# Key low parts zero-padded to 128 rows in the score matmuls of a differential attention

## The chip, the cores and the metric

The kernel runs on one core of a Trainium2 chip. The metric is the device time of one execution in microseconds (us), as the median over runs: 940.03 us for the kernel before, from 3 runs between 939.41 and 940.34.

## What is computed

One hybrid decoder layer in float32, with 512 tokens and a model width of 2048. One input projection feeds three branches: differential attention (8 heads), a state space mixer and an attention into 256 memory tokens. Their gated outputs go through one output projection, a norm and the residual. The change touches the differential attention. Each head has two components c of 64 query and key features, and 128 value features:

```python
s = einsum('bhcqd,bhckd->bhcqk', q_blk, k) * 64 ** -0.5     # c = 0, 1; d = 64
p = softmax(where(causal, s, -inf), axis=-1)
a = p[:, :, 0] - lam * p[:, :, 1]
o = einsum('bhqk,bhkv->bhqv', a, v)
o = rms_norm(o, diff_subln_w) * (1.0 - lambda_init)
```

## The kernel before, in words

Every large product is made in a reduced-precision float32 form (fp32r): each operand is split into a high part that fits the form and a low part that holds the rest, and three matmuls (high by high, high by low, low by high; the helper `mm3`, L95 to L97) give the product. Weights come from memory as chunks of 512 KB by the SP queue (`load_chunk`, L215). ScalarE makes the high part (L247, tile `whi`), VectorE subtracts it from the chunk to make the low part (`sub_hi`, L100, tile `wlo`). Three raw chunks and two split ones are held at a time. `dense_ws` makes one block of 128 output features by 512 tokens in 48 matmuls of 512 columns; `dense_xs` makes the values `v` with matmuls of 256 columns.

The differential attention works on four pairs of heads. For each pair the values, then two blocks q and two blocks k are projected. `rope` (L738 and below) rotates a block: ScalarE copies it out of PSUM into `raw` (L740), four small transfers on the SP queue fetch the swapped halves into `sw` (L743), GpSimd (POOL) multiplies both by the tables (L744, L745), and VectorE adds them (L746). The result is then laid out in a tile `pair` of two slots, one per component. For q, slot c holds in one half of the 128 rows the high part of component c and in the other half its low part. For k, both halves of slot c hold the high part of component c, half of them copied by POOL (L755, L756). So one matmul over 128 rows (L777) makes q-high by k-high and q-low by k-high together. What is missing is q-high by k-low. Before the change, `kl` holds the low parts of both components in one tile of 512 columns, component 0 in rows 0 to 63 and component 1 in rows 64 to 127, and a second matmul over those 64 rows (L780) adds it to the same PSUM bank.

In `head`, the score tile of query block i (i = 0 to 3) and component c has (i+1)*128 columns. So one head has eight L777 matmuls and eight L780 matmuls, two of each width 128, 256, 384 and 512, and the eight heads have 64 of each. After them VectorE masks and finds the maximum (L781, L782), ScalarE takes the exponential (L787), VectorE normalises and combines the two components (L790 to L793), TensorE transposes (L797), and the result is split (L798, L100) for the product with v (tile `av`). The tail of a head copies `av` out (L807), takes the sum of squares and scales.

The order of the instructions on each engine is set when the program is built, by a scheduler that interleaves independent work: the score matmuls of one pair of heads stand singly or in small groups between the projection matmuls of the next pair (`v`, `q`, `k`), and those of the last pair between the projections of the gates (`dg`).

Of the kernel before, what the change touches and what calls it, by code (L numbers as in the profile page):

```python
# [11 lines left out]
F32 = mybir.dt.float32  # L12
F32R = mybir.dt.float32r
BF16 = mybir.dt.bfloat16
I32 = mybir.dt.int32
AF = mybir.ActivationFunctionType
ALU = mybir.AluOpType
AX = mybir.AxisListType
PSUM = bass.MemoryType.PSUM

P = 128
D = 2048
S = 512
# [13 lines left out]


def _digits(value, widths):
    """value as a sum of float32 parts of the given numbers of bits."""  # L40
    from fractions import Fraction
    out, rest = [], Fraction(value)
    for w in widths:
        if rest == 0:
            out.append(0.0)
            continue
        e = math.floor(math.log2(float(abs(rest))))
        unit = Fraction(2) ** (e - w + 1)
        part = Fraction(math.floor(rest / unit)) * unit
        out.append(float(part))  # L50
        rest -= part
    return out
# [16 lines left out]
def hymba_kernel(ctx: ExitStack, tc: tile.TileContext, x, mem, positions, pre_norm_w, w_in,  # L69
# [20 lines left out]
    def ft(pool, shape, tag, name, bufs=None, dt=F32):  # L90
        kw = {} if bufs is None else {"bufs": bufs}
        return pool.tile(shape, dt, tag=tag, name=name, **kw)
# [6 lines left out]
    def sub_hi(lo, src, hi):  # L99
        nc.vector.tensor_tensor(lo, src, hi.bitcast(F32), ALU.subtract)  # L100

# [1 line left out]
    nc.scalar.preload_act_table_set("natural_log_exp_and_others")  # L103
    ident = const.tile([P, P], F32, name="ident")
    make_identity(nc, ident)
# [46 lines left out]
    nc.gpsimd.memset(ones, 1.0)  # L152

    def col_sums(ps, src, func, scale, sq, upper, parts):
        """ps = sums of func(scale * src) over all partitions."""
        a, b = slice(0, 64), slice(64, 128)
        nc.scalar.activation(sq[a], src[a], func, scale=scale)
        nc.scalar.activation(upper[a], src[b], func, scale=scale)
        nc.vector.tensor_tensor(sq[a], sq[a], upper[a], ALU.add)
        nc.scalar.activation(parts[a], sq[a], AF.Copy)  # L160
        sub_hi(parts[b], sq[a], parts[a])
        nc.tensor.matmul(ps, ones_r, parts, start=True, stop=True)

# [1 line left out]
    chunks = []  # L165

    def plan(w, col0, ncols, nkt, dt_cols=None):
# [117 lines left out]
        return ps  # L285

    def neg2_rstd(y, t, v):
        """y = -2 / sqrt(v + EPS), with one Newton step; t is scratch, v may be in PSUM."""
        nc.scalar.activation(t, v, AF.Ln, bias=epsc)
        nc.scalar.activation(y, t, AF.Exp, scale=-0.5)  # L290
        nc.vector.tensor_tensor(t, y, y, ALU.mult)
        nc.vector.scalar_tensor_tensor(t, v, EPS, t, ALU.add, ALU.mult)
        nc.vector.scalar_tensor_tensor(y, t, 3.0, y, ALU.subtract, ALU.mult)
# [3 lines left out]
    def push(name, side="right"):  # L297
        cm = tc.tile_pool(name=name, bufs=1, side=side, reuse_waits="tile")
        open_pools.append(cm)
        return cm.__enter__()  # L300
# [5 lines left out]
    mkv = push("mkv", "left")  # L306
    st = push("stage", "left")

# [1 line left out]
    def exp_table():  # L310
        tc.keep_in_program_order(
            nc.scalar.preload_act_table_set("natural_log_exp_and_others"))
# [98 lines left out]
    tab = push("tab")  # L411
    vp = push("vp")

# [1 line left out]
    sml = const.tile([P, 32], F32, name="sml")  # L415
    nc.sync.dma_start(sml[:, 0:8], dt_bias[0].partition_broadcast(P))
    nc.sync.dma_start(sml[:, 8:16], a_log[0].partition_broadcast(P))
# [45 lines left out]
    nc.scalar.activation(dte, dte, AF.Exp)  # L463
    nc.scalar.activation(cdec, alast, AF.Exp)

# [1 line left out]
    xp = push("xp", "left")  # L467
    xo = []
    XSC = 128 ** -0.5
# [42 lines left out]
            nc.scalar.activation(o, po, AF.Copy)  # L512
            xo.append(o)

# [1 line left out]
    for cm in (open_pools.pop(), open_pools.pop(1)):  # L516
        cm.__exit__(None, None, None)
    sp = push("sp")
# [138 lines left out]
            nc.vector.tensor_scalar(zs[i], zs[i], vcol("sn", i), -0.5, ALU.mult, ALU.mult)  # L657
            nc.vector.tensor_tensor(zs[i], zs[i], ry, ALU.mult)

# [1 line left out]
    rc = const.tile([P, 2], F32, name="rc")  # L661
    nc.sync.dma_start(rc, rope_cols)
    cosT = ft(tab, [P, S], "cosT", "cosT")
# [44 lines left out]
            nc.gpsimd.dma_start(cosT[dst, ts], ang[src])  # L708
            nc.gpsimd.dma_start(sinT[dst, ts], (t2 if b % 2 else turn)[src])

# [1 line left out]
    lt = ft(sp, [P, 4, 64], "lt", "lt")  # L712
    for i, l in enumerate((lambda_q1, lambda_q2, lambda_k1, lambda_k2)):
        nc.sync.dma_start(lt[:, i], l[0].partition_broadcast(P))
# [7 lines left out]
    subc = const.tile([P, 1], F32, name="subc")  # L722
    nc.vector.tensor_scalar(subc, vcol("sub", 0), 1.0 - LAMBDA_INIT, -0.5, ALU.mult, ALU.mult)

# [1 line left out]
    for c in range(2):  # L726
        for i in range(2):
            ps = dense_ws(hT, S, f"xg{c}{i}")
# [3 lines left out]
        exp_table()  # L732
    pop()

# [1 line left out]
    ap = push("ap")  # L736

    def rope(psb, kind, h):  # L738
        raw = ft(ap, [P, S], "raw", f"raw_{kind}{h}", 2)
        nc.scalar.activation(raw, psb, AF.Copy)  # L740
        sw = ft(ap, [P, S], "sw", f"sw_{kind}{h}", 2)
        for b in range(4):
            nc.sync.dma_start(sw[32 * b:32 * b + 32], raw[32 * (b ^ 1):32 * (b ^ 1) + 32])  # L743
        nc.gpsimd.tensor_tensor(raw, raw, cosT, ALU.mult)  # L744
        nc.gpsimd.tensor_tensor(sw, sw, sinT, ALU.mult)  # L745
        nc.vector.tensor_tensor(raw, raw, sw, ALU.add)  # L746
        a, b = slice(0, 64), slice(64, 128)
        pair = ft(ap, [P, 2, S], kind + "2", f"{kind}2_{h}", 2, F32R)
        nc.scalar.activation(pair[a, 0], raw[a], AF.Copy)
        nc.scalar.activation(pair[b, 1], raw[b], AF.Copy)  # L750
        if kind == "q":
            sub_hi(pair[b, 0], raw[a], pair[a, 0])
            sub_hi(pair[a, 1], raw[b], pair[b, 1])
            return pair
        nc.gpsimd.tensor_scalar(pair[b, 0], raw[a], 1.0, 1.0, ALU.mult, ALU.mult)  # L755
        nc.gpsimd.tensor_scalar(pair[a, 1], raw[b], 1.0, 1.0, ALU.mult, ALU.mult)  # L756
        low = ft(ap, [P, S], "kl", f"kl{h}", 2, F32R)
        sub_hi(low[a], raw[a], pair[a, 0])
        sub_hi(low[b], raw[b], pair[b, 1])
        return pair, low  # L760

    DSC = 64 ** -0.5
# [2 lines left out]
    def head(h, q, k, v):  # L765
        k2, kl = k
        vh, vl = v
        vs = slice((h % 2) * P, (h % 2 + 1) * P)
        aTh = ft(ap, [P, NT, S], "aTh", f"aTh{h}", 1, F32R)
        aTl = ft(ap, [P, NT, S], "aTl", f"aTl{h}", 1, F32R)  # L770
        for i in range(NT):
            w = (i + 1) * P
            qs = slice(i * P, w)
            sc = [bank("sc", f"sc{h}{i}{c}") for c in range(2)]
            nm = ft(small, [P, 2], "nm", f"nm{h}{i}")
            for c in range(2):
                nc.tensor.matmul(sc[c][:, :w], q[:, c, qs], k2[:, c, :w], start=True, stop=False)  # L777
            for c in range(2):
                ds_ = slice(c * 64, (c + 1) * 64)
                nc.tensor.matmul(sc[c][:, :w], q[ds_, c, qs], kl[ds_, :w], start=False, stop=True)  # L780
                nc.vector.tensor_tensor(sc[c][:, qs], sc[c][:, qs], cmask, ALU.add)  # L781
                nc.vector.tensor_reduce(nm[:, c:c + 1], sc[c][:, :w], AX.X, ALU.max, negate=True)  # L782
            nc.vector.tensor_scalar(nm, nm, DSC, None, ALU.mult)  # L783
            ls = ft(small, [P, 2], "ls", f"ls{h}{i}")
            pc = [ft(ap, [P, S], f"p{c}", f"p{h}{i}{c}", 2 - c) for c in range(2)]
            for c in range(2):
                nc.scalar.activation(pc[c][:, :w], sc[c][:, :w], AF.Exp, bias=nm[:, c:c + 1],  # L787
                                     scale=DSC, accum_out=ls[:, c:c + 1])
            rl = ft(small, [P, 2], "rl", f"rl{h}{i}")
            nc.vector.reciprocal(rl, ls)  # L790
            nc.vector.tensor_scalar(rl[:, 1:2], rl[:, 1:2], nlam, None, ALU.mult)
            nc.vector.tensor_scalar(pc[0][:, :w], pc[0][:, :w], rl[:, 0:1], None, ALU.mult)
            nc.vector.scalar_tensor_tensor(pc[0][:, :w], pc[1][:, :w], rl[:, 1:2], pc[0][:, :w],  # L793
                                           ALU.mult, ALU.add)
            tp = bank("tr", f"atr{h}{i}").rearrange("p (j q) -> p j q", j=NT)
            for j in range(i + 1):
                nc.tensor.transpose(tp[:, j], pc[0][:, j * P:(j + 1) * P], ident)  # L797
            nc.scalar.activation(aTh[:, :i + 1, qs], tp[:, :i + 1], AF.Copy)  # L798
            sub_hi(aTl[:, :i + 1, qs], tp[:, :i + 1], aTh[:, :i + 1, qs])
        po = bank("av", f"av{h}")  # L800
        for j in range(NT):
            qs = slice(j * P, S)
            mm3(po[:, qs], vh[:, j, vs], vl[:, j, vs], aTh[:, j, qs], aTl[:, j, qs],
                j == 0, j == NT - 1)
        osb = ft(ap, [P, S], "osb", f"osb{h}", 1)
        osq = ft(ap, [P, S], "osq", f"osq{h}", 1)
        nc.scalar.activation(osb, po, AF.Copy)  # L807
        mp = bank("av", f"oms{h}")
        col_sums(mp, po, AF.Square, 128 ** -0.5, osq, ft(ap, [P, S], "ory", f"oup{h}", 1),
                 ft(ap, [P, S], "p1", f"osp{h}", 1, F32R))  # L810
        ry = ft(ap, [P, S], "ory", f"ory{h}", 1)
        neg2_rstd(ry, osq, mp)
        o = ft(slots_p, [P, S], f"s{h}", f"do{h}")
        nc.vector.scalar_tensor_tensor(o, osb, subc, ry, ALU.mult, ALU.mult)
        do.append(o)

    for p in range(4):
# [16 lines left out]
    for _ in range(3):  # L834
        pop()

# [1 line left out]
    ep = push("ep")  # L838
    pw = ft(ep, [P, D], "pw", "pw")
    nc.sync.dma_start(pw, post_norm_w[0].partition_broadcast(P))  # L840
# [84 lines left out]
```

## Time and profile before

| what | value |
|---|---|
| median of 3 runs | 940.03 us |
| lowest and highest run | 939.41 us, 940.34 us |
| span of the profiled execution (first to last instruction) | 938.0 us |
| TensorE matmul (PE) busy | 919.9 us, 98% |
| TensorE weight load (PEld) busy | 767.7 us, 82% |
| VectorE (DVE) busy | 520.8 us, 56% |
| ScalarE (ACT) busy | 426.4 us, 45% |
| GpSimd (POOL) busy | 118.3 us, 13% |

The profile gives no time for the profiled execution apart from its span; the span is 2.03 us (0.2%) under the median of the runs. A busy time of PE says that a matmul was in flight. Matmuls overlap, each record runs from the start of the matmul to its modelled end, and so the distance from one start to the next start tells what a matmul occupies, not its duration.

### The profile page before, as it was taken

Reading aid. Unit: us, or ns where it says so; the run is one execution under the profiler, and the core shown is the slowest. Engines: PE = TensorE matmul, PEld = TensorE weight load, DVE = VectorE, ACT = ScalarE, POOL = GpSimd, SP = SyncE. Lnnn points to the kernel's source line nnn. Section 1 sums busy time; section 2 is a strip of 40 time slices with the busy share of each in tenths; the row PEclk is TensorE's granted clock in tenths of the full one; section 3 lists DMA queues with packets and bytes.
Section 4 is the critical chain, followed back from the end, with each engine's and each line's share of the span. In section 5 each row is a group of like instructions: output and inputs, shape, how many; then the busy total and the mean of one; then the engine's idle time right before and its main releaser. Section 6 shows DMA issues by size and latency. Waiting matters only on the chain.

```text
span 938.0 us, 12534 instructions
## 1 busy us (share of the span) xinstructions
PE 919.9 (98%) x4794; PEld 767.7 (82%) x4794; DVE 520.8 (56%) x974; ACT 426.4 (45%) x705; POOL 118.3 (13%) x130
## 2 busy tenths in 40 slices
PE   7899999999999999999999999999999999999996
PEld 5799888888888888888788789878777878888896
DVE  5574555594576423474886677486646553232345
ACT  4753244454365733344453444454756753122331
POOL 2310000006000111311220111014110110000000
PEclk9999999999999999999999999999999999999999
DMA  6962322444352333423422333333222252222227
GB/s 223 339 172 80 90 68 69 135 120 113 89 136 68 92 107 94 122 81 79 113 79 81 100 91 86 83 83 97 81 76 81 89 226 90 92 98 102 90 68 269
DMA packets 137093, 104.42 MB, mean 111 GB/s; under 512 B 8693, under 2 KB 121026, under 8 KB 136394
## 3 DMA queue, kind: packets, MB, share of 16 engines
q1 hardware_dynamic: 136010, 103.11, 37.4%
q8 instruction: 37, 0.61, 0.3%
q0 software_dynamic: 1024, 0.53, 0.2%
q14 instruction: 22, 0.18, 0.1%
HBM read 94.68 MB, written 4.21 MB: 105 GB/s over the span
## 4 chain that ended last, share of the span: by engine, by line
PE 93%; DMA 3%; ACT 1%; DVE 1%; issue 0%; SPq 0%; POOL 0%; DVEq 0%; POOLq 0%
PE wo L96 6%; PE wo L97 6%; PE wo L95 6%; PE v L97 4%; PE v L95 3%; PE v L96 3%; PE k L97 3%; PE q L96 3%; PE q L95 3%; PE k L95 3%; PE q L97 3%; PE k L96 3%; PE xbc L96 3%; PE xbc L97 3%; PE xbc L95 3%; PE dg L97 3%
## 5 line engine op out<-in xcount | busy, mean ns | idle before, releaser
L100 DVE TENSOR_TENSOR wlo<-raw,whi 128x1024 fp32r<-128x1024 f32 (+2 forms) x149 | 188.6, 1266 | 223.2 <-ACT whi L247 209.4
L247 ACT ACTIVATE whi<-raw 128x1024 fp32r<-128x1024 f32 (+1 forms) x132 | 139.8, 1059 | 225.1 <-PE wo L97 89.0
L96 PE MATMUL wo<-wlo,mxh 128*128 128x512 f32 (+1 forms) x256 | 93.3, 365 | 0.0
L97 PE MATMUL wo<-whi,mxl 128*128 128x512 f32 (+1 forms) x256 | 93.1, 364 | 0.0
L95 PE MATMUL wo<-whi,mxh 128*128 128x512 f32 (+1 forms) x256 | 81.8, 366 | 0.9 <-ACT dgate L831 0.9
L97 PE MATMUL v<-whi,hTl 128*128 128x256 f32 (+1 forms) x256 | 74.1, 291 | 0.0
L96 PE MATMUL v<-wlo,hTh 128*128 128x256 f32 (+1 forms) x256 | 73.1, 286 | 0.0
L95 PE MATMUL v<-whi,hTh 128*128 128x256 f32 (+1 forms) x256 | 72.8, 286 | 0.0
L787 ACT ACTIVATE p<-sc,nm 128x128 f32<-128x128 f32 (+3 forms) x64 | 33.3, 524 | 60.7 <-DVE nm L783 56.6
L95 PEld LDWEIGHTS wo<-whi,mxh 128*128 128x128 f32 x256 | 48.0, 188 | 9.9 <-ACT dgate L831 1.4
L96 PEld LDWEIGHTS wo<-wlo,mxh 128*128 128x128 f32 x256 | 48.2, 188 | 8.3
L97 PEld LDWEIGHTS wo<-whi,mxl 128*128 128x128 f32 x256 | 48.2, 188 | 8.0
L97 PE MATMUL k<-hTh,wlo 128*128 128x512 f32 x128 | 51.2, 400 | 0.0
L97 PE MATMUL dg<-hTh,wlo 128*128 128x512 f32 x128 | 51.2, 400 | 0.0
L95 PE MATMUL q<-hTh,whi 128*128 128x512 f32 x128 | 51.1, 399 | 0.0
L96 PE MATMUL dg<-hTl,whi 128*128 128x512 f32 x128 | 51.0, 398 | 0.0
L96 PE MATMUL q<-hTl,whi 128*128 128x512 f32 x128 | 50.9, 398 | 0.0
L96 PE MATMUL k<-hTl,whi 128*128 128x512 f32 x128 | 50.9, 397 | 0.0
L95 PE MATMUL dg<-hTh,whi 128*128 128x512 f32 x128 | 50.8, 397 | 0.0
L97 PE MATMUL xbc<-hTh,wlo 128*128 128x512 f32 x128 | 50.7, 396 | 0.0
L96 PE MATMUL xbc<-hTl,whi 128*128 128x512 f32 x128 | 50.6, 395 | 0.0
L95 PE MATMUL k<-hTh,whi 128*128 128x512 f32 x128 | 50.6, 395 | 0.0
(327 smaller groups left out, 2136.9 us busy)
## 6 DMA issues: line engine op xcount, KB each, us to landing
raw<-in_w_in_dram SPq DMA_DIRECT2D x104, 512.0 KB, 3.7
raw<-in_w_out_dram SPq DMA_DIRECT2D x32, 512.0 KB, 3.4
raw<-in_w_mem_kv_dram SPq DMA_DIRECT2D x15, 512.0 KB, 6.2
x_rows<-in_x_dram SPq DMA_DIRECT2D x8, 512.0 KB, 7.3
xr<-in_x_dram SPq DMA_DIRECT2D x4, 1024.0 KB, 5.3
out_dram<-oacc SPq DMA_DIRECT2D x12, 256.0 KB, 3.1
mem_rows<-in_mem_dram SPq DMA_DIRECT2D x8, 256.0 KB, 5.5
dm<-act_d SPq DMA_DIRECT2D x8, 256.0 KB, 4.1
```

Source lines behind the costliest of these rows:

```text
L95: nc.tensor.matmul(ps, ah, bh, start=start, stop=False)
L96: nc.tensor.matmul(ps, ah, bl, start=False, stop=False)
L97: nc.tensor.matmul(ps, al, bh, start=False, stop=stop)
L100: nc.vector.tensor_tensor(lo, src, hi.bitcast(F32), ALU.subtract)
L247: nc.scalar.activation(hi[:, :n], raw[:, :n], AF.Copy)
L787: nc.scalar.activation(pc[c][:, :w], sc[c][:, :w], AF.Exp, bias=nm[:, c:c + 1], scale=DSC, accum_out=ls[:, c:c + 1])
```

## The change

The low parts of the keys get two tiles, `klow0` and `klow1`, one for heads of even and one for heads of odd number. Each has two slots of 512 columns, one per component. Their unused halves are set to zero once, by four memsets on POOL, and stay zero; per head only the 64 rows of the component are written, by the same two subtractions on VectorE as before. The matmul of the low part then takes the whole 128 rows of q's slot c and of `klow`'s slot c: the rows that hold q-low meet zeros.

Two other tiles shrink or go: `sw` has one buffer and not two, and the copy of `av` goes straight to the head's output slot (`do`), where it is scaled in place, so that the tile `osb` is gone. The remaining lines of the diff remove comments.

```diff
     ap = push("ap")
+    klows = []
+    for e in range(2):
+        low = ft(ap, [P, 2, S], f"klow{e}", f"klow{e}", 1, F32R)
+        nc.gpsimd.memset(low[64:128, 0].bitcast(F32), 0.0)
+        nc.gpsimd.memset(low[0:64, 1].bitcast(F32), 0.0)
+        klows.append(low)
...
-        sw = ft(ap, [P, S], "sw", f"sw_{kind}{h}", 2)
+        sw = ft(ap, [P, S], "sw", f"sw_{kind}{h}", 1)
...
-        low = ft(ap, [P, S], "kl", f"kl{h}", 2, F32R)
-        sub_hi(low[a], raw[a], pair[a, 0])
-        sub_hi(low[b], raw[b], pair[b, 1])
+        low = klows[h % 2]
+        sub_hi(low[a, 0], raw[a], pair[a, 0])
+        sub_hi(low[b, 1], raw[b], pair[b, 1])
...
-                ds_ = slice(c * 64, (c + 1) * 64)
-                nc.tensor.matmul(sc[c][:, :w], q[ds_, c, qs], kl[ds_, :w], start=False, stop=True)
+                nc.tensor.matmul(sc[c][:, :w], q[:, c, qs], kl[:, c, :w], start=False, stop=True)
...
-        osb = ft(ap, [P, S], "osb", f"osb{h}", 1)
+        o = ft(slots_p, [P, S], f"s{h}", f"do{h}")
         osq = ft(ap, [P, S], "osq", f"osq{h}", 1)
-        nc.scalar.activation(osb, po, AF.Copy)
+        nc.scalar.activation(o, po, AF.Copy)
...
-        o = ft(slots_p, [P, S], f"s{h}", f"do{h}")
-        nc.vector.scalar_tensor_tensor(o, osb, subc, ry, ALU.mult, ALU.mult)
+        nc.vector.scalar_tensor_tensor(o, o, subc, ry, ALU.mult, ALU.mult)
```

On POOL, between the last gate product of the memory attention and the first rotation, the kernel before has:

```order
L731 TENSOR_TENSOR xo_1549<-xo_1549,xgate_3086 128x512
L731 TENSOR_TENSOR xo_1675<-xo_1675,xgate_3150 128x512
L744 TENSOR_TENSOR raw_q_3219<-raw_q_3219,cosT 128x512
L745 TENSOR_TENSOR sw_q_3221<-sw_q_3221,sinT 128x512
L744 TENSOR_TENSOR raw_q_3295<-raw_q_3295,cosT 128x512
```

and the changed kernel, whose lines from L738 on are numbered six higher:

```order
L731 TENSOR_TENSOR xo_1549<-xo_1549,xgate_3086 128x512
L731 TENSOR_TENSOR xo_1675<-xo_1675,xgate_3150 128x512
L740 MEMSET klow_3158 64x512
L741 MEMSET klow_3158 64x512
L740 MEMSET klow_3161 64x512
L741 MEMSET klow_3161 64x512
L750 TENSOR_TENSOR raw_q_3225<-raw_q_3225,cosT 128x512
L751 TENSOR_TENSOR sw_q_3227<-sw_q_3227,sinT 128x512
L750 TENSOR_TENSOR raw_q_3301<-raw_q_3301,cosT 128x512
```

The four memsets are the only instructions that are new on any engine; the others keep their order on all of them. On PE, for the third query block of head 0 (tile numbers differ, the order is the same), the changed kernel has:

```order
L96 MATMUL v_1_3761<-wlo_3765,hTh_545 128x256
L783 MATMUL sc_3528<-k_0_3387,q_0_3235 128x384
L785 MATMUL sc_3528<-klow_3158,q_0_3235 128x384
L97 MATMUL v_1_3761<-whi_3764,hTl_546 128x256
L95 MATMUL v_1_3761<-whi_3764,hTh_545 128x256
```

Each low-part matmul still stands right behind the high-part matmul of its bank. On the SP queue, what a transfer waits for is in brackets. At the second rotation of the first pair the kernel before has:

```order
L743 DMA sw_q_3297<-raw_q_3295 32x512 [waits Activation_49]
L743 DMA sw_q_3297<-raw_q_3295 32x512 [waits DMAHW2_49]
L743 DMA sw_q_3297<-raw_q_3295 32x512 [waits DMAHW3_49]
L743 DMA sw_q_3297<-raw_q_3295 32x512 [waits DMAHW4_49]
L215 DMA raw_3390<-in_w_in_dram 128x4x256 [waits DMAHW5_49,DVE_49]
```

and the changed kernel:

```order
L749 DMA sw_q_3303<-raw_q_3301 32x512 [waits DMAHW4_49,DMAHW5_49,DMAHW3_49,DMAHW6_49,DVE_49,Activation_49]
L749 DMA sw_q_3303<-raw_q_3301 32x512 [waits DMAHW2_49]
L749 DMA sw_q_3303<-raw_q_3301 32x512 x2
L215 DMA raw_3395<-in_w_in_dram 128x4x256 [waits DVE_49]
L215 DMA raw_3425<-in_w_in_dram 128x4x256 [waits DMAHW7_49,DVE_49]
```

The swap of one rotation now also waits for VectorE, which must have added the previous rotation's `sw`, and the weight chunks stand behind it on the same queue.

## Rows read from the trace of the kernel before

**Rows 1.** Page, parts 1 and 4: span, busy time by engine, the chain that ended last.

```profile
span 938.0 us, 12534 instructions
...
PE 919.9 (98%) x4794; PEld 767.7 (82%) x4794; DVE 520.8 (56%) x974; ACT 426.4 (45%) x705; POOL 118.3 (13%) x130
...
PE 93%; DMA 3%; ACT 1%; DVE 1%; issue 0%; SPq 0%; POOL 0%; DVEq 0%; POOLq 0%
```

**Rows 2.** Stretch 520 to 590 us: length, busy PE, PEld, DVE, ACT, POOL, clock, DMA.

```profile
520.00:590.00 70.00, 70.00 (x400) 58.71 (x399) 52.20 (x107) 35.06 (x70) 13.51 (x12) 1.00 0.34 91
```

**Rows 3.** All instructions on tile `kl`: duration min/median/max; idle before them, times.

```profile
L780 PEld LDWEIGHTS sc<-kl,q x64: 182/183/183, 393.0 to 717.4; 64*128 64x128 f32 x64
L780 PE MATMUL sc<-kl,q x64: 322/409/503, 393.0 to 717.4; 64*128 64x128 f32 x16, 64*128 64x256 f32 x16, 64*128 64x384 f32 x16, 64*128 64x512 f32 x16
...
  issue: 11.9, 45
```

**Rows 4.** Timeline of PE: start, duration, instruction; a 128-wide score matmul alone.

```profile
558.35 0.23 PE L777 MATMUL sc<-k,q 128*128 128x128 f32 x1
558.41 0.34 PE L97 MATMUL v<-whi,hTl 128*128 128x256 f32 x1
558.58 0.28 PE L95 MATMUL v<-whi,hTh 128*128 128x256 f32 x1
558.70 0.28 PE L96 MATMUL v<-wlo,hTh 128*128 128x256 f32 x1
```

**Rows 5.** Timeline of PE: low-part matmuls of 128 and of 256 columns.

```profile
416.62 0.22 PE L777 MATMUL sc<-k,q 128*128 128x128 f32 x1
416.78 0.33 PE L780 MATMUL sc<-kl,q 64*128 64x128 f32 x1
417.03 0.39 PE L95 MATMUL v<-whi,hTh 128*128 128x256 f32 x1
417.25 0.28 PE L96 MATMUL v<-wlo,hTh 128*128 128x256 f32 x1
...
417.73 0.28 PE L777 MATMUL sc<-k,q 128*128 128x256 f32 x1
417.94 0.38 PE L780 MATMUL sc<-kl,q 64*128 64x256 f32 x1
418.25 0.39 PE L97 MATMUL v<-whi,hTl 128*128 128x256 f32 x1
418.47 0.28 PE L95 MATMUL v<-whi,hTh 128*128 128x256 f32 x1
```

**Rows 6.** Timeline of PE: a low-part matmul of 512 columns among projections of 512.

```profile
448.78 0.40 PE L777 MATMUL sc<-k,q 128*128 128x512 f32 x1
449.11 0.49 PE L780 MATMUL sc<-kl,q 64*128 64x512 f32 x1
449.53 0.50 PE L97 MATMUL k<-hTh,wlo 128*128 128x512 f32 x1
449.87 0.40 PE L95 MATMUL k<-hTh,whi 128*128 128x512 f32 x1
450.10 0.39 PE L96 MATMUL k<-hTl,whi 128*128 128x512 f32 x1
```

**Rows 7.** Timeline of POOL around the place of the memsets.

```profile
348.35 1.85 POOL L731 TENSOR_TENSOR xo<-xo,xgate 128x512 f32<-128x512 f32 x1 [8.33 <-ACT xgate L730]
364.27 1.29 POOL L744 TENSOR_TENSOR raw_q<-raw_q,cosT 128x512 f32<-128x512 f32 x1 [14.07 <-DMA sw_q<-raw_q]
```

**Rows 8.** Timeline of DVE and of SP: the second rotation's addition, the third's swaps.

```profile
379.08 0.69 DVE L746 TENSOR_TENSOR raw_q<-raw_q,sw_q 128x512 f32<-128x512 f32 x1 [2.44 <-POOL sw_q L745]
...
382.74 2.41 SPq L743 DMA_DIRECT2D sw_k<-raw_k  x4
```

**Rows 9.** Timeline of ACT and PE: an exponential, and the matmul that reuses its bank.

```profile
486.25 0.37 ACT L787 ACTIVATE p<-sc,nm 128x128 f32<-128x128 f32 x1
...
487.84 0.33 PE L777 MATMUL sc<-k,q 128*128 128x384 f32 x1
```

## The prediction

> **What bounds the kernel now.** I read the page first. TensorE's matmuls are in flight for 919.9 of 938.0 us, and the chain of waits that ended last runs through PE for 93% of its length [rows 1]. So time is won only where PE itself takes less, and lost only where something makes PE wait. The table by stretches tells whether that holds in the attention, where the change lies: from 520 to 590 us PE is busy for all of the 70 us, at a granted clock of 1.00 (the upper level, 2.4 GHz), while DVE, the next busiest, has 52.2 us of work [rows 2]. The view of tile `kl` then shows the 64 matmuls that the change rewrites: they are recorded as tiles of 64 rows by 128 columns (`64*128`), 16 of each width, and the weight load sat idle before 45 of them, 11.9 us in all, with nothing that it waited for [rows 3]. The reader is to see that idle time as a sign, not as the cost: the cost shows in the distances between starts on PE.
>
> **What a low-part matmul occupies.** First the normal pace, from places with no 64-row tile. From 558.35 to 558.70 us stand one score matmul of 128 columns and two projections of 256, 0.35 us; the last two starts are 0.12 us apart [rows 4]. So 256 columns occupy 0.12 us and 128 columns 0.35 - 2 x 0.12 = 0.11 us.
>
> Now the same with a 64-row matmul between. I count from the start of L777 to the start of the second ordinary matmul behind L780, since the first ordinary one is stretched too:
>
> - 128 columns: 416.62 to 417.25, 0.63 us for work of 0.11 + 0.11 + 0.12 = 0.34 us. Excess 0.29 us [rows 4, 5].
> - 256 columns: 417.73 to 418.47, 0.74 us for 3 x 0.12 = 0.36 us. Excess 0.38 us [rows 4, 5].
> - 512 columns: two ordinary projections start 0.23 us apart (449.87 to 450.10); 448.78 to 449.87 is 1.09 us for 3 x 0.23 = 0.69 us. Excess 0.40 us [rows 6].
>
> The excess lies in three places: L777 to L780 about 0.1 us more than the width needs, L780 to the next 0.2 us more, and that one again 0.1 us more. It hardly grows with the width, so it belongs to going in and out of the 64-row tile, not to the columns.
>
> **The change part by part.**
>
> *128 rows for the low part.* This takes the way in and out away. The order of PE's instructions has 64 low-part matmuls; at four places two of them stand next to each other (a 128-wide one before a 256-wide one) and share one way in and out. That leaves 60 passages: 12 of 128 columns, 4 shared ones that I price like 128 columns, 12 of 256, 16 of 384, which I price like 512, and 16 of 512. The sum is 16 x 0.29 + 12 x 0.38 + 32 x 0.40 = 4.6 + 4.6 + 12.8 = 22.0 us. The trace has no 128-row low-part matmul, so what one will occupy is bounded: by a normal start distance of its width, as I take it (the L777 matmul alone in [rows 4] is nearest to it, same stationary tile, same bank, same rows), or at the cheap end 0.06 us for 128 columns, the distance from 558.35 to 558.41 [rows 4]. That would give 0.05 us more at some 32 matmuls, 1.6 us. At the dear end it occupies what the 64-row one does, and nothing is won.
>
> Here a rule stands against the change. The rows show excess at every width for the 64-row tile [rows 5, 6]. The Trainium skill, "TensorE: Matmul & The Clock Gate", in the table of "Why this matters for your kernels", says that a single matmul over 32 rows takes the same time as one over 128, and that the gain of few rows is that tiles of different rows run at once. By it this edit is worth 0 us, and loses a little where two low parts stand side by side; by the rows it is worth 22.0 us. The traces price the step from one tile shape to another, which that rule leaves aside, so I go by the rows.
>
> *Zeros in the other half.* Four memsets of 64x512 on POOL, once. POOL finished its last product before that place at 350.20 us and was idle for 14.07 us until 364.27 [rows 7]. A POOL operation over twice the rows takes 1.29 us there, so four cost at most 4 x 1.29 = 5.2 us and end some 9 us early: 0 us. Without that cover they would delay the first rotation by 5.2 us. The subtractions that write `klow` are the same two per head: 0 us.
>
> *One buffer for `sw`.* The swap transfers of a rotation now wait until VectorE has added the previous one. Within each pair of heads that is three swaps, 12 in all. In the first pair the second addition ended at 379.77 us and the third swap was issued at 382.74, 2.97 us later [rows 8]; in the other gaps it is as much or more, give or take 0.1 us. The memsets come earlier and do not move it. A faster PE shortens such a gap by the passages that fall into it, at most two or three (0.8 to 1.2 us). So the new wait is met before it is reached: 0 us. If that slack were gone, the SP queue would hold the weight chunks behind it.
>
> *No `osb`.* ScalarE writes the same 128x512 to another tile, and the scaling reads it there: 0 us, and one reuse wait fewer.
>
> *What is late next.* With PE some 6% faster through 330 us, its partners have less time. The tightest I found is a score matmul at 487.84 us whose bank the exponential of 486.25 freed at 486.62: 1.22 us of slack [rows 9]; the others have that or more, apart from matmuls behind POOL's copies of k, which no passage precedes closely. One or two passages lie inside such a loop, and take 0.4 to 0.8 us off. That leaves it just open. DVE would have 52.2 us of work in about 65 instead of 70 us [rows 2], 80%. I put 0.5 us of new waits into the sum; the bounds are 0, and 8 us, if a third of the passages win nothing because PE waits for the bank instead.
>
> **The sum.** -22.0 + 0.5 = -21.5 us. The profiled span would go from 938.0 to 916.5 us. The median of the runs lies 2.03 us above that span, so 940.03 - 21.5 = 918.5 us.
>
> **The rivals.**
>
> *PE wins the passages, and waits instead.* The loop score, mask, exponential, bank becomes the limit in parts of the attention. For it: slacks of 1.2 us, and DVE at 80%. Against it: DVE and ACT did not hold PE up in any of the attention's stretches, and the loop contains few passages. With 2 to 8 us lost: 920.0 to 926.0 us. Chance 0.15.
>
> *The number of rows is not what costs.* The excess is then due to two matmuls in a row on one score bank with a fresh stationary tile, or to reading freshly written low parts, and stays: 940.0 us. This is also what the rule of the page named above gives. Against it: projections also follow each other on one bank at 0.23 us [rows 6], and the excess is there behind L780 too, where the next matmul shares nothing with it [rows 5]. The Trainium skill itself has the opposite rule in "TensorEngine Tiling (Array Packing)", "Key Properties", where a change of tiling mode drains the engine; the trace agrees with that one, by 0.29 to 0.40 us at each passage [rows 5, 6]. Chance 0.04.
>
> *Slower: the single `sw`.* The swap on the SP queue waits for the addition, the weight chunks wait behind the swap, and ScalarE and PE run out of weights. It decides only from the point where an addition ends 2.97 us later than now [rows 8]. To come out above 942 us it must cost 24 us, 2 us at each of the 12 swaps beyond that slack and beyond the chunks already loaded. Nothing in the profile puts additions that late: POOL has 13.5 us of work in 70 [rows 2]. Some 943 us. Chance 0.02.
>
> That the change might not do what it says is excluded for the order: on PE no instruction moves.
>
> **How the numbers follow.** The forecast has 0.79 and is the predicted time, 918.5 us. Its lower end is 1.6 us from cheaper 128-wide matmuls and 0.5 us without new waits: 916.4, and I set 916.0 for the spread of the runs. The upper end takes in 6 of the 8 us of new waits: 924.5 us. Left out are about 0.04 of the waiting case, 0.06 of the two others and some 0.06 below. Runs of this kernel lie within 0.1% of each other, so 0.2% (1.9 us) is about what can be told from no change. Faster by more than that: 0.94, the first two cases. Within it: 0.04. Slower: 0.02.
>
> **What would show it.** The low-part matmuls should be recorded as `128*128`, with no "issue" idle before their weight loads. In the timeline, L783 (the former L777), L785 and the next matmul should start at the pace of their widths, 0.23 us each at 512 columns, and the stretch from 390 to 736 us should be some 21 us shorter with PE still busy throughout. Wrong would be: the same distances at 128 rows (the second rival); score matmuls or transposes of PE waiting for ACT or DVE with several us in all (the first); SP's swaps waiting for VectorE, and ScalarE waiting for chunks (the third).

## The result, and the profile after

The changed kernel takes 918.54 us (median of 4 runs, 918.23 to 919.15), the kernel before 939.82 us in the same comparison (4 runs, 939.41 to 940.34). The ratio is 0.9772, with a 95% interval from 0.9758 to 0.9786: 21.3 us less. The forecast was 918.5 us. The profiled execution took 918.23 us, with a span of 916.5 us, which is the span that the sum of the prediction gave.

The page after, parts 1 and 4, answers to [rows 1]:

```profile
span 916.5 us, 12561 instructions
...
PE 898.5 (98%) x4794; PEld 767.4 (84%) x4794; DVE 519.7 (57%) x974; ACT 425.2 (46%) x705; POOL 123.4 (13%) x134
...
PE 90%; DMA 3%; ACT 2%; DVE 2%; SPq 1%; POOL 1%; issue 1%; DVEq 0%; POOLq 0%; ACTq 0%
```

PE has as many matmuls as before and is in flight for 21.4 us less; the work of the other engines is the same within some 1 us, but for POOL: its four memsets take 2.1 us, and its other instructions, the same in number, some 3 us more than before. The chain still runs through PE.

All instructions on the tile of the low parts, against [rows 3]:

```profile
L785 PEld LDWEIGHTS sc<-klow,q x64: 186/188/193, 392.6 to 696.2; 128*128 128x128 f32 x64
L785 PE MATMUL sc<-klow,q x64: 222/333/397, 392.6 to 696.5; 128*128 128x128 f32 x16, 128*128 128x256 f32 x16, 128*128 128x384 f32 x16, 128*128 128x512 f32 x16
```

They are full tiles (`128*128`), and the 11.9 us that the weight load idled for "issue" are gone from the list. One weight load takes 5 ns longer. The timeline of PE at the places of [rows 5] and [rows 6]: start, duration, instruction.

```profile
413.57 0.23 PE L783 MATMUL sc<-k,q 128*128 128x128 f32 x1
413.63 0.27 PE L785 MATMUL sc<-klow,q 128*128 128x128 f32 x1
413.74 0.34 PE L95 MATMUL v<-whi,hTh 128*128 128x256 f32 x1
413.91 0.28 PE L96 MATMUL v<-wlo,hTh 128*128 128x256 f32 x1
...
414.39 0.28 PE L783 MATMUL sc<-k,q 128*128 128x256 f32 x1
414.51 0.28 PE L785 MATMUL sc<-klow,q 128*128 128x256 f32 x1
414.63 0.28 PE L97 MATMUL v<-whi,hTl 128*128 128x256 f32 x1
414.74 0.28 PE L95 MATMUL v<-whi,hTh 128*128 128x256 f32 x1
...
443.88 0.39 PE L783 MATMUL sc<-k,q 128*128 128x512 f32 x1
444.11 0.40 PE L785 MATMUL sc<-klow,q 128*128 128x512 f32 x1
444.34 0.39 PE L97 MATMUL k<-hTh,wlo 128*128 128x512 f32 x1
444.57 0.40 PE L95 MATMUL k<-hTh,whi 128*128 128x512 f32 x1
```

From L783 to the second ordinary matmul it is now 0.34, 0.35 and 0.69 us, where it was 0.63, 0.74 and 1.09 us, and 0.34, 0.36 and 0.69 us were taken as the normal pace. Nothing of the excess is left at these three widths. PE's order is the same in both traces, so the other passages can be set side by side too: the 16 of 384 columns are each 0.38 to 0.40 us shorter, and all 60 together 21.7 us.

What goes on at a passage shows in the weight loads (PEld), at the place of [rows 6]. Before:

```profile
449.10 0.18 PEld L780 LDWEIGHTS sc<-kl,q 64*128 64x128 f32 x1 [0.36 <-issue]
449.53 0.19 PEld L97 LDWEIGHTS k<-hTh,wlo 128*128 128x128 f32 x1 [0.24 <-DVE q L100]
449.63 0.19 PEld L95 LDWEIGHTS k<-hTh,whi 128*128 128x128 f32 x1
```

After:

```profile
443.88 0.19 PEld L785 LDWEIGHTS sc<-klow,q 128*128 128x128 f32 x1
```

At the normal pace a load starts one matmul ahead, at 443.88 us for the matmul at 444.11. The load of the 64-row tile (449.10) and that of the first full tile behind it (449.53) start only with their own matmuls (449.11 and 449.53); the one after them is ahead again (449.63 for 449.87).

To see whether the time went there and nowhere else, I read one stretch in both traces, from the first score matmul to the first one of the output projection (columns as in [rows 2]). Before:

```profile
392.36:749.24 356.88, 356.88 (x1839) 291.10 (x1837) 236.10 (x476) 182.46 (x340) 55.48 (x48) 1.00 0.31 86
```

After:

```profile
392.23:728.05 335.82, 335.54 (x1839) 290.11 (x1837) 232.61 (x476) 181.34 (x340) 58.57 (x48) 1.00 0.35 91
```

The same number of instructions of every engine takes 335.82 in place of 356.88 us, 21.06 of the span's 21.5 us. The clock is at its upper level in both.

### The profile page after: what moved, and what is told of

It reads as the page before. It is cut to its first block, busy times and chain, and to the rows that moved or that the text cites. A ratio compares the mean times of both kernels' runs of the same rounds, so it can differ in the third digit from the quotient of the medians.

```text
span 916.5 us, 12561 instructions
## 1 busy us (share of the span) xinstructions
PE 898.5 (98%) x4794; PEld 767.4 (84%) x4794; DVE 519.7 (57%) x974; ACT 425.2 (46%) x705; POOL 123.4 (13%) x134
## 4 chain that ended last, share of the span: by engine, by line
PE 90%; DMA 3%; ACT 2%; DVE 2%; SPq 1%; POOL 1%; issue 1%; DVEq 0%; POOLq 0%; ACTq 0%
PE wo L96 6%; PE wo L97 6%; PE wo L95 6%; PE v L97 3%; PE v L95 3%; PE v L96 3%; PE q L95 3%; PE q L96 3%; PE q L97 3%; PE xbc L96 3%; PE xbc L97 3%; PE xbc L95 3%; PE k L96 3%; PE k L95 3%; PE k L97 3%; PE dg L96 2%
## 5 line engine op out<-in xcount | busy, mean ns | idle before, releaser
L97 PE MATMUL q<-hTh,wlo 128*128 128x512 f32 x128 | 50.4, 394 | 0.0
```

Of the source, the lines that this page charges most:

```text
L97: nc.tensor.matmul(ps, al, bh, start=False, stop=stop)
```

## The experiments

The theory: each time PE goes from a tile of 128 rows into one of 64 and back, it pays 0.29 to 0.40 us, whatever the 64-row matmul computes. The rivals: the other edits made the gain; a 64-row matmul is slower per column; the excess needs something of the scores (their bank, q's stationary tile, freshly written keys).

**Only the rows undone.** In the changed kernel:

```diff
-                nc.tensor.matmul(sc[c][:, :w], q[:, c, qs], kl[:, c, :w], start=False, stop=True)
+                ds_ = slice(c * 64, (c + 1) * 64)
+                nc.tensor.matmul(sc[c][:, :w], q[ds_, c, qs], kl[ds_, c, :w], start=False, stop=True)
```

> The changed kernel with one thing undone: the low-part matmul takes the 64 rows of its component again, out of the zero-padded tiles. Memsets, the single sw buffer and the head's output slot stay as changed, and so does the order on every engine. If the way in and out of the 64-row tile is the cost (0.29 to 0.40 us at 60 passages), all of the gain goes: 940 us, at most 1 us off, and the idle time before the weight loads of the low part is back (some 12 us over some 45 of 64). If the other edits made the gain, it stays at 918.5 us. If the number of rows costs half of it, some 929 us.

It took 940.24 us (ratio to the kernel before 1.0003, interval 0.9994 to 1.0012). All of the gain is gone. The instructions on `klow` show the old tile and the old idle time:

```profile
L786 PE MATMUL sc<-klow,q x64: 322/409/503, 393.4 to 717.8; 64*128 64x128 f32 x16, 64*128 64x256 f32 x16, 64*128 64x384 f32 x16, 64*128 64x512 f32 x16
...
  issue: 11.9, 45
```

The rows of this one matmul are the whole of the change's effect; memsets, tiles and order are as in the changed kernel.

**The other edits alone.** In the kernel before:

```diff
-        sw = ft(ap, [P, S], "sw", f"sw_{kind}{h}", 2)
+        sw = ft(ap, [P, S], "sw", f"sw_{kind}{h}", 1)
...
-        osb = ft(ap, [P, S], "osb", f"osb{h}", 1)
+        o = ft(slots_p, [P, S], f"s{h}", f"do{h}")
...
-        nc.scalar.activation(osb, po, AF.Copy)
+        nc.scalar.activation(o, po, AF.Copy)
```

> The kernel before with only the other edits: one buffer for sw, and the copy of av straight into the head's output slot. The low part stays as it was, 64 rows of one tile of 512 columns. If these edits cost and win nothing, as the prediction had it, 939.8 us within 0.2% (938 to 941.7). If the single buffer costs something that the change's gain covers, above 942 us, with waits of SP for VectorE; if dropping osb wins something, under 938 us.

It took 939.99 us, ratio 1.0000 (0.9991 to 1.0009). One buffer for `sw` and the missing `osb` neither cost nor win anything that can be measured.

**64 rows for one width only.** Two kernels, the changed one with the old matmul for query block 3 (512 columns) or for query block 0 (128 columns). The edit of the first; the other has `i == 0`:

```diff
-                nc.tensor.matmul(sc[c][:, :w], q[:, c, qs], kl[:, c, :w], start=False, stop=True)
+                rows = slice(c * 64, (c + 1) * 64) if i == 3 else slice(0, P)
+                nc.tensor.matmul(sc[c][:, :w], q[rows, c, qs], kl[rows, c, :w], start=False, stop=True)
```

> The changed kernel, with 64 rows again only for the 16 low-part matmuls of 512 columns (query block 3). If the cost is one per passage, 16 x 0.40 = 6.4 us come back: 918.5 + 6.4 = 924.9 us. If a 64-row matmul is slower per column, this block has 4 of every 10 columns, and 0.4 x 21.3 = 8.5 us come back: 927.0 us. If rows do not matter, 918.5 us.

It took 925.58 us (924.65 to 926.68), 7.0 us over the changed kernel; the spans of the two profiled executions differ by 922.9 - 916.5 = 6.4 us. By the spans that is one price per passage, 16 x 0.40; the median lies between the two expectations, 924.9 and 927.0 us. So this run alone does not exclude a cost per column. The narrow one does:

> The changed kernel, with 64 rows again only for the 16 low-part matmuls of 128 columns (query block 0). One of ten columns of the low part is in this block. If the cost is one per passage, 16 x 0.29 = 4.6 us come back: 918.5 + 4.6 = 923.1 us. If a 64-row matmul is slower per column, 0.1 x 21.3 = 2.1 us: 920.7 us. If rows do not matter, 918.5 us.

It took 923.22 us (923.0 to 923.49), 4.7 us over the changed kernel and 2.5 us over what a cost per column gives. A quarter of the columns costs seven tenths as much: the price is one per passage, 0.29 us at 128 columns.

**Two 64-row matmuls in one passage.** On top of the first experiment, the low-part matmuls of a query block stand next to each other:

```diff
             for c in range(2):
                 ds_ = slice(c * 64, (c + 1) * 64)
-                nc.tensor.matmul(sc[c][:, :w], q[ds_, c, qs], kl[ds_, c, :w], start=False, stop=True)
+                tc.keep_in_program_order(
+                    nc.tensor.matmul(sc[c][:, :w], q[ds_, c, qs], kl[ds_, c, :w],
+                                     start=False, stop=True))
+            for c in range(2):
                 nc.vector.tensor_tensor(sc[c][:, qs], sc[c][:, qs], cmask, ALU.add)
```

> As the first kernel of this call (64 rows out of the padded tiles), but the two low-part matmuls of a query block are pinned behind both high-part matmuls, one after the other; the mask of component 0 comes later for that. By its order on PE, 64 low-part matmuls stand in 36 groups (28 pairs, 8 alone) in place of 60. If each way in and out costs 0.29 to 0.40 us, 24 fewer of them win 9 us: 931 us. If moreover the two of a pair, on different rows, run at once, each pair hides one of them (0.11 to 0.23 us), some 4 us more: 927 us. If the passages are not the cost, 940 us. New waits for a score bank, since both must be free at once, can add 1 to 3 us.

It took 925.67 us (925.49 to 926.18): 14.6 us less than with single ones, somewhat more than the 13 us that fewer passages and overlap gave together. The waits for a score bank that were thought possible do not appear in its trace. Its instructions stand in another order on PE, so this total is a less exact comparison than the others. The timeline of PE at a pair of 512 columns (`x2` is the pair):

```profile
456.12 0.39 PE L783 MATMUL sc<-k,q 128*128 128x512 f32 x1
456.44 0.51 PE L787 MATMUL sc<-klow,q 64*128 64x512 f32 x2
456.88 0.50 PE L95 MATMUL k<-hTh,whi 128*128 128x512 f32 x1
457.21 0.40 PE L96 MATMUL k<-hTl,whi 128*128 128x512 f32 x1
```

From the pair to the next matmul it is 0.44 us; for one 64-row matmul of 512 columns it was 0.42 us [rows 6]. So the two, on different rows and in different banks, run at once. The Trainium skill, "TensorE: Matmul & The Clock Gate", "Part 3: Packing small matmuls — row/col tiling", says that tiles of different rows overlap, and this trace agrees. But the way in and out is still paid: the four matmuls take 456.12 to 457.21, 1.09 us, and four of 128 rows would take 4 x 0.23 = 0.92 us. Even in pairs, 64 rows lose at this width. Larger groups would need more score banks than the three there are, and were not tried.

**The cost by itself.** The changed kernel, with a matmul by zeros added in 32 chunks of the projections for the state space mixer and the memory gate, far from the scores:

```diff
+    zero_r = ft(sp, [P, P], "zero_r", "zero_r", 1, F32R)
+    nc.gpsimd.memset(zero_r.bitcast(F32), 0.0)
+    zeros.append(zero_r)
...
+                if name[0] in "xz" and name[:2] != "xq" and kk == 4:
+                    rows = slice(0, 64)
+                    nc.tensor.matmul(ps[:, :n], zeros[0][rows], xh[rows], start=False, stop=False)
```

> The cost measured by itself, away from the scores: the changed kernel with one matmul of 512 columns added in each of 32 chunks of the projections xbc, z and xg. Its stationary tile is 64 rows of zeros, so that it adds nothing. If it pays its columns and one way in and out, 32 x (0.23 + 0.40) = 20.2 us: 938.7 us. If the excess needs a score bank, q's stationary tile or freshly written keys, only the columns are paid, 32 x 0.23 = 7.4 us: 925.9 us. If zero operands are free, 918.5 us.

The control has `slice(0, P)` for the rows:

> The same as the kernel with 64 inserted rows, in the same order, but with 128 rows of zeros: the control for it. 32 x 0.23 = 7.4 us by both theories: 925.9 us. If it comes out as long as the one with 64 rows, the excess is not that of the 64 rows.

They took 945.56 us (945.47 to 946.09) and 934.08 us (933.59 to 934.51). Both lie 7 to 8 us above the expectation, but their difference, 11.5 us or 0.36 us for each inserted matmul (12.5 us or 0.39 by the spans), is close to the expected 0.40. The level is off for a reason outside the question, told in the last section. The stretch from the first z matmul to the first q matmul has no such disturbance and holds 16 of the inserted ones. The same columns as above, for the changed kernel:

```profile
244.55:346.63 102.08, 102.08 (x500) 83.59 (x499) 53.21 (x82) 56.45 (x65) 10.71 (x9) 1.00 0.38 98
```

with 128 inserted rows:

```profile
256.70:362.49 105.79, 105.79 (x516) 86.64 (x515) 52.41 (x82) 56.43 (x65) 11.66 (x9) 1.00 0.36 95
```

and with 64:

```profile
262.85:374.86 112.01, 112.01 (x516) 85.37 (x515) 52.42 (x82) 56.36 (x65) 11.63 (x9) 1.00 0.34 90
```

The control adds 3.71 us, 0.23 for each: its columns, zeros or not. With 64 rows it is 6.22 us more, 0.39 us for each. The timeline of PE with 64 inserted rows shows the three places where it is paid:

```profile
328.65 0.39 PE L97 MATMUL xg<-hTh,wlo 128*128 128x512 f32 x1
328.97 0.50 PE L271 MATMUL xg<-hTh,zero_r 64*128 64x512 f32 x1
329.39 0.50 PE L95 MATMUL xg<-hTh,whi 128*128 128x512 f32 x1
329.73 0.39 PE L96 MATMUL xg<-hTl,whi 128*128 128x512 f32 x1
```

0.32, 0.42 and 0.34 us, in place of 0.23 each: 0.1, 0.2 and 0.1 us, as at the scores. No score bank, no q and no key is near. This closes the rival that needed something of the scores.

None of these kernels beats the changed one, and no run pointed to a version that would.

## Why the prediction was right

*What bounds the kernel.* It took PE to be the bound through the whole attention, so that every us that PE saves there is a us of the run. The stretch from the first score to the output projection became 21.06 us shorter, with PE busy for 335.54 of 335.82 us.

*128 rows for the low part, -22.0 us.* The normal pace was the right price for the matmul to come: 0.34, 0.35 and 0.69 us measured, 0.34, 0.36 and 0.69 us used. The excess per passage was also right as a price for putting it back, 4.7 us for 16 narrow ones (4.6 expected), 6.4 us by the spans for 16 wide ones (6.4). The cheap end, 128-wide matmuls at 0.06 us, did not come true: the row pair at 413.57 and 413.63 us is 0.06 us apart, but the next two distances, 0.11 and 0.17 us, take it back.

*New waits, +0.5 us.* One wait appeared where the step on what is late next had looked for it: a score matmul for its bank. It is not the one that was tightest before, though, but one in the last pair of heads. PE and ACT there:

```profile
646.26 0.39 PE L95 MATMUL dg<-hTh,whi 128*128 128x512 f32 x1
646.93 0.50 PE L783 MATMUL sc<-k,q 128*128 128x512 f32 x1 [0.28 <-ACT p L792]
...
644.50 1.28 ACT L290 ACT_TABLE_LOAD   x1
645.80 0.63 ACT L290 ACTIVATE ory<-osq 128x512 f32<-128x512 f32 x1
646.33 0.46 ACT L792 ACTIVATE p<-sc,nm 128x256 f32<-128x256 f32 x1
```

The distance is 0.67 in place of 0.23 us, 0.44 us lost. The exponential that had to free the bank stood behind two other activations on ACT and the loading of a function table ahead of each of them (`ACT_TABLE_LOAD`, at 642.59 and 644.50 us, 1.28 us each). ACT had the same order before the change. Before, this bank had hardly more to spare than the 1.22 us of the one that the prediction named: 1.27 us, since its exponential ended at 663.49 us, and the matmul started at 664.76.

```profile
663.03 0.46 ACT L787 ACTIVATE p<-sc,nm 128x256 f32<-128x256 f32 x1
...
664.76 0.39 PE L777 MATMUL sc<-k,q 128*128 128x512 f32 x1
```

After the change, 0.23 us behind the matmul of 646.26, PE would have been there at 646.49 us, 0.30 us before the exponential ended at 646.79. So PE gained 1.57 us on it, about four passages, where the prediction allowed one or two (0.4 to 0.8 us); at the bank of [rows 9] it gained 0.28 us (1.22 us of slack became 0.94). That step had the kind of wait right, but not how much of a slack goes. That 0.5 us met 0.44 is luck: the figure was set, not worked out, and with another bank in mind. The rival of 2 to 8 us of new waits did not happen.

*Zeros in the other half, 0 us.* The last of the four memsets on POOL and what follows it, against [rows 7]:

```profile
351.82 0.52 POOL L741 MEMSET klow<- 64x512 f32 x1
363.42 1.29 POOL L750 TENSOR_TENSOR raw_q<-raw_q,cosT 128x512 f32<-128x512 f32 x1 [11.08 <-DMA sw_q<-raw_q]
```

The memsets end 11 us before POOL's next work. A memset of 64 rows took 0.52 us, the bound used was 1.29.

*One buffer for `sw`, and no `osb`, 0 us.* By their own run, nothing. The second addition now ends at 379.12 us and the third swap is issued at 382.04, 2.92 us later, where it was 2.97 us [rows 8]:

```profile
378.43 0.69 DVE L752 TENSOR_TENSOR raw_q<-raw_q,sw_q 128x512 f32<-128x512 f32 x1 [1.18 <-POOL sw_q L751]
...
382.04 2.42 SPq L749 DMA_DIRECT2D sw_k<-raw_k  x4
```

The rival that came out slower is thereby excluded.

*The number of rows is not what costs (chance 0.04).* It fell with the first experiment. The rule of the Trainium skill, "TensorE: Matmul & The Clock Gate", "Why this matters for your kernels", that a single matmul of few rows takes as long as one of many, does not hold for a 64-row matmul in this stream: the measured 0.29 to 0.40 us decide. Whether it holds among matmuls of one tile shape, no run here shows. The rule of the Trainium skill, "TensorEngine Tiling (Array Packing)", "Key Properties", that a change of tiling mode drains the engine, agrees with these distances; which part of a passage is drain and which is a weight load that does not run ahead was not separated.

The sum has no term that was off by more than 0.5 us: -22.0 + 0.5 in the prediction, -21.5 in the span, -21.3 by the medians. That it met the span to 0.1 us is in part luck. Only 21.06 us of the 21.5 lie in the stretch that the change touches; the span also lost 0.13 us ahead of it and 0.31 us behind it, which belong to no term of the sum.

## What to carry to other kernels

In a dense stream of full-tile matmuls like this one, a single matmul over 64 rows cost 0.29 to 0.40 us more than one over 128 rows padded with zeros, because of the tiles on either side of it. Pad it if the zeros can be laid down once, or put 64-row matmuls on different rows side by side and count whether the overlap pays the way in and out. The price is read from distances between starts, up to the second matmul behind. The busy time of the rewritten matmuls (25.0 us before, 19.9 after) and the recorded idle time of their weight loads (11.9 us) each show only a part of the 22 us; PE's busy time as a whole (21.4 us less) shows nearly all of it.

## What was not expected

The inserted zeros made a kernel slower by 15.5 us where their columns take 7.4. The trace of the one with 128 rows has PE waiting in the memory attention, which the changed kernel does not do (us in total, times, longest us):

```profile
PE xtr L506 <- DVE xpt L502: 2.1, 1, 2.1
PE xtr L506 <- DVE pTl L100: 1.5, 1, 1.5
PE xav L95 <- ACT pTh L509: 0.7, 1, 0.7
```

and behind these waits a slower clock (columns as above, the granted clock third from the end):

```profile
150.00:160.00 10.00, 6.05 (x35) 4.54 (x33) 4.70 (x13) 3.92 (x12) 0.20 (x1) 0.93 0.25 59
160.00:170.00 10.00, 9.65 (x33) 7.17 (x34) 4.32 (x11) 1.95 (x3) 0.00 (x0) 0.73 0.09 28
```

PE was idle for some 4 us, and then had the lower of its two clock levels (1.2 GHz) for a part of the next 10. The trace shows why PE had nothing to do: after the one that starts at 150.57 us no projection matmul starts on PE until 164.08, while in the changed kernel projections stand between the matmuls of the memory attention (at 153.12 us, for example). So the inserted matmul changed PE's order as it is set when the program is built; the zero tile was not what PE waited for, since its memset began at 152.77 us and took 0.20. My reading, which no run tests, is that the scheduler holds the projections back because the zero tile is made only behind the memory attention in the program. An experiment that adds a tile can move the schedule by more than the cost it is to measure; the control, in the same order, is what made it readable.
